# A recurrence's triangular inverses: systems on two partitions instead of one, and a load held back

## The chip, the cores and the metric

The kernel runs on one core of a Trainium2 chip. The core has a matrix engine (TensorE, PE in the rows), a vector engine (VectorE, DVE), an engine for activation functions and copies (ScalarE, ACT), a general one (GpSimd, POOL) and a queue engine that issues most DMAs (SyncE, SP). The metric is the device time of one execution in microseconds. Times of before: 2339.28 us, the median of 3 runs from 2338.95 to 2339.99.

## The reference, cut to what matters

The program is a decoder trunk of two layers with D = 2048 and T = 272 positions (256 and 16 learned ones): an RWKV-7 time mixing, a squared-ReLU MLP, a gated linear attention, another MLP. The change lies in the first mixer, whose recurrence over the positions is, for each of 32 heads of 64:

```python
def rwkv7_scan(r, w, k, v, a, b):
    def step(S, inp):
        r_t, w_t, k_t, v_t, a_t, b_t = inp
        sa = jnp.einsum('bhvk,bhk->bhv', S, a_t)
        S = S * w_t[:, :, None, :] + sa[..., None] * b_t[:, :, None, :] + v_t[..., None] * k_t[:, :, None, :]
        y = jnp.einsum('bhvk,bhk->bhv', S, r_t)
        return S, y
...
out = ((y + bonus).astype(x.dtype) * g) @ w_o
```

Around it stand projections of 2048 by 2048: keys and values before it, the output projection behind it.

## The kernel before, in words

The recurrence is computed in chunks of 64 positions (four, and a short fifth), in two groups of 16 heads. In a chunk, the positions depend on one another through a triangular system with a unit diagonal, for each head. `scores` (L956 on TensorE, masked on VectorE at L719 into a tile AM) makes these systems, and stores their diagonal blocks of 32 by 32 to DRAM (`sysd`, L963). `invert(b)`, b = 0 to 3, loads a batch of them into `sysA`, one system on each partition (L982: 64 of them for b = 0 and 2; 80 for b = 1 and 3, which have the short chunk too), and inverts all at once on VectorE in 30 steps. A step has two operations, both through the helper of L719: `upd` gets the product of a column and a row, and is then added into `sysA`. Step s works on s rows of 31 − s columns. Afterwards the inverses are stored (`invd`, L993), four transposes (L995, STREAM_TRANSPOSE) put some of them into `t11`, a part of `sysA`'s own tile, and loads from `invd` (L1000) put the rest into AM. `merge` joins two blocks of 32 to an inverse of 64 on TensorE (L1126, L1136).

All this runs beside projections that fill TensorE: each float32 product is split in three passes (L173 to L175), with a weight tile `raw` loaded by SyncE (`wload`, L141), rounded to `hi` by ScalarE (L150), and subtracted to `lo` by VectorE (L151), here in two halves of 512 columns. A pass with `lo` can't start before this subtraction. `R(n)` lets n units of the projections run (one unit is three matmuls), `until(n)` runs them up to a count, `MARK` holds the counts at which an inverse has to be there. `some(inv, n)` advances an inverse by n steps in the program's text.

The order on TensorE is that of the text (`manual_schedule`). That on the other engines is made by the framework's scheduler from its own costs, with priorities that the text gives (`high_priority`), so an inverse's steps are dealt out among VectorE's other work. Each engine then runs its instructions strictly in that order.

In the first inverse, `rest(f)` (L1044 on) prepares the keys of 128 channels, f = 0 to 15: decayed operands `bk` and `ar`, in two buffers each, are stored to DRAM (`bkd`, `ard`, L1008), and a buffer can be rewritten when its store has landed. `sums` (L1023) adds squares over channels on TensorE. The first inverse runs with f = 13, 14, 15 and the first value projections. The second group's start has the fourth inverse: `centre(1, 0)` puts the centred values `uv` (L1157), `norm` (L1247 to L1282) normalizes what came out of the first group, `outQ` adds partial sums of the output projection from psum into `r` and `hres` (`r<-pj` in the rows).

Of the kernel before, what the change touches and what calls it, by code (L numbers as in the profile page):

```python
# [13 lines left out]
ALU = mybir.AluOpType  # L14
# [4 lines left out]
P = 128  # L19
# [42 lines left out]
class Kern:  # L62
# [654 lines left out]
    def rwkv(self, done):  # L717
        nc, tc, ap = self.nc, self.tc, self.ap
        tt = lambda o, a, b, op=ALU.mult: nc.vector.tensor_tensor(out=o, in0=a, in1=b, op=op)  # L719
        hres = self.hres  # L720
# [5 lines left out]
        sysd, invd = ([self.t(self.dp, [112, 32, 32], f"{n}{b}") for b in range(4)] for n in ("sysd", "invd"))  # L726
# [27 lines left out]
        def hl(mt, xm):  # L754
            nc.scalar.copy(mt[:, 0], xm)
            tt(mt[:, 1], xm, mt[:, 0].bitcast(F32), ALU.subtract)
# [28 lines left out]
        with tc.manual_schedule(engines={ENG.PE, ENG.DVE, ENG.Activation}):  # L785
            for _ in range(2):
                nc.tensor.matmul(idle, warm[:, :128], warm[:, :512], start=True, stop=True)
            for i in range(8):
                sq, h = self.t(ep, [P, 2, T], "x", KT), d[:, 2 * i : 2 * i + 2]
# [8 lines left out]
            w = warm.bitcast(F32R)  # L798
            x, o = self.weave(w[:, :512]), self.pairs(idle)
# [37 lines left out]
            for kt in range(KT):  # L837
                w = weight(kt)
# [14 lines left out]
                p = parts.pop(0)  # L853
# [117 lines left out]

        def invert(b):
            X = sysA
            n = P if b % 2 else 64
            some_rows = [slice(0, 64), slice(96, 112)][: 1 + b % 2]
            if b % 2:
                nc.gpsimd.memset(X[64:96], 0.0)
            for rows in some_rows:  # L980
                with tc.high_priority(offset=4000):
                    nc.sync.dma_start(X[rows], sysd[b][rows])  # L982
            nc.gpsimd.memset(X[:n].rearrange("p a b -> p (a b)")[:, ::33], 1.0)
            yield
            for s in range(1, 31):
                k, m = 31 - s, s
                w = self.t(lp, [P, 240], "upd", 1)[:n, : k * m].rearrange("p (a b) -> p a b", a=m)
                tt(w, X[:n, s : s + 1, s + 1 :].to_broadcast([n, m, k]), X[:n, :m, s : s + 1].to_broadcast([n, m, k]))
                tt(X[:n, :m, s + 1 :], X[:n, :m, s + 1 :], w, ALU.add)
                yield  # L990
            for rows in some_rows:
                with tc.high_priority(offset=4000):
                    nc.sync.dma_start(invd[b][rows], X[rows])  # L993
            for k in (slice(8 * i, 8 * i + 8) for i in range(4)):
                nc.vector.transpose(t11.rearrange("p c h s -> p s c h")[:, k], X[0:32, k])  # L995
                yield
            for c in ((2, 3, 4) if b % 2 else (0, 1)):
                for rows, x in reversed(blocks(c, slice(0, 16))):
                    with tc.high_priority(offset=4000):
                        nc.sync.dma_start(x, invd[b][rows].rearrange("h s t -> s h t"))  # L1000
# [71 lines left out]
        with tc.manual_schedule(engines={ENG.PE}):  # L1072
            for f in range(KT):
                ps = (self.pry if f % 3 == 2 else self.pj)()[:, :T]
                keyproj(f, ps, 0)
                if f:
                    with tc.high_priority(offset=600):
                        rest(f - 1)
                keyproj(f, ps, 1)
                front(f, ps)  # L1080
                if f == 1:
                    xv = [self.t(self.xp, [P, 2, T], "x", KT, F32R) for _ in range(KT)]
                    for kt in range(KT):
                        hl(xv[kt], d[:, kt])
                    early2.close()
                    wl = ExitStack()
                    lp = wl.enter_context(tc.tile_pool(name="wl", bufs=1, reuse_waits="tile"))
                    BKs, ARs = ([self.t(lp, [P, 8, 256], n)] for n in ("BK0", "AR0"))
                    BKs.append(self.t(lp, [P, 8, 320], "BK1"))
                    AMs, AMrs = [self.t(lp, [P, 2, 16, 128], "AM0")], []  # L1090
                    sysA = self.t(lp, [P, 32, 32], "sysA")
                    t11 = sysA.rearrange("p a b -> p (a b)")[64:96].rearrange("p (c h s) -> p c h s", c=2, h=16)
                    nc.gpsimd.memset(sysA, 0.0)
                if f in (5, 6, 7):
                    dst, src, i, j = ((BKs[0], bkd, 0, 256), (ARs[0], ard, 0, 256), (BKs[1], bkd, 256, 576))[f - 5]
                    nc.sync.dma_start(dst[:, :4], src[:4, :, i:j].rearrange("f p n -> p f n"))
                if 8 < f < 13:
                    scores(0, (f - 9) // 2, (f + 1) % 2)
                if f == 12:
                    inv = invert(0)  # L1100
                if f > 12:
                    for _ in range(6):
                        next(inv, None)

        bank = lambda x: x.rearrange("p (h v) -> p h v", h=8)
        uvs, ras, bkts, rys, pSs = {}, {}, {}, {}, {}
# [39 lines left out]
        def centre(g, c):  # L1146
            full, n, nr = geom(c)[:3]
            pv = self.pm()
            for p in range(4):
                for e in range(2):  # L1150
                    nc.tensor.matmul(pv[64 * e : 64 * e + nr, p * P : (p + 1) * P], hres[:, 8 * g + 4 * e + p, c * C : c * C + nr],
                                     self.cent, start=True, stop=True)
            x = uvs[g, c] = self.t(kp, [P, 16, 64], "uv", 2)
            if not full:
                nc.gpsimd.memset(x[0 : 2 * n], 0.0)
            for e in range(2):
                nc.scalar.copy(x[:nr, 8 * e : 8 * e + 8], pv[64 * e : 64 * e + nr].rearrange("p (h v) -> p h v", h=8))  # L1157
# [219 lines left out]
        def R(n):  # L1377
            for _ in range(n):
                if next(work, work) is not work:
                    ran[0] += 1  # L1380
# [4 lines left out]
        def some(it, n):  # L1385
            for _ in range(n):
                next(it, None)
# [3 lines left out]
        self.split_parts = 2  # L1391
        ahead()
        with tc.manual_schedule(engines={ENG.PE}):
            R(4)
            with tc.high_priority(offset=600):
                rest(KT - 1)
            R(12)
            sums(None)
        early.close()

# [1 line left out]
        kp = win.enter_context(tc.tile_pool(name="win", bufs=1, side="right", reuse_waits="tile"))  # L1402
        ARs.append(self.t(kp, [P, 8, 320], "AR1"))
        AMs.append(self.t(kp, [P, 2, 16, 128], "AM1"))
        AMrs.append(self.t(kp, [64, 16, 64], "AMr"))
        sb = self.t(kp, [P, 8, HEAD], "S")
        for i in ((0, 128), (128, 320)):
            fetch(1, ARs, ard, i)
        with tc.manual_schedule(engines={ENG.PE}):
# [5 lines left out]
            for g in range(2):  # L1415
# [12 lines left out]
                m = merge(2 * g)  # L1428
# [1 line left out]
                some(last, 1)  # L1430
                R(4)
                next(m)
                inv = invert(2 * g + 1)
                some(inv, 3)
                until(128 + 128 * g)
                centre(g, 0)
                some(last, 1)
                R(2)
                keys(g, 0)
# [7 lines left out]
                for c in range(5):  # L1447
                    if c == 2:
# [5 lines left out]
                        m = merge(2 * g + 1)  # L1454
# [25 lines left out]
                    if g == 0 and c == 2:  # L1480
                        scores(2, 1, 1)
                        inv = invert(2)
# [351 lines left out]
```

## Time and profile before

| | us |
|---|---|
| median of 3 runs | 2339.28 |
| profiled execution | 2338.84 |
| its span | 2337.0 |
| TensorE busy in it | 2309.4 (99%) |
| VectorE busy | 1827.2 (78%) |
| ScalarE busy | 1381.9 (59%) |
| GpSimd busy | 311.8 (13%) |

The table is read against the bound: an engine that is busy for 99% of the span leaves little to be won, and only where it waits. The averages of the other engines say little of one stage: VectorE, at 78% of the whole, is nearly full in parts of the recurrence (about 240 to 500 us). A wait is given in brackets behind the instruction that waited, with the instruction that ended it.

### The profile page before, as it was taken

The numbers are of one execution on the slowest core, as the hardware profiler recorded it, in microseconds if no ns is written. First come the engines' busy times: TensorE is split into PE (matmuls) and PEld (weight loads), VectorE is DVE, ScalarE is ACT, GpSimd is POOL, SyncE is SP. The second block draws the span as 40 slices with busy tenths as digits, with TensorE's granted clock in tenths as the row PEclk, the third lists the DMA queues.
The fourth block names the chain that finished last, engine by engine and source line by source line (L and its number), as shares of the span: only waits on it lengthen the run. The fifth ranks groups of instructions, "written<-read, shape, count | busy, mean of one in ns | idle before, by whom it ended". The sixth has DMA issues, their size and how long they took to land.

```text
span 2337.0 us, 49154 instructions
## 1 busy us (share of the span) xinstructions
PE 2309.4 (99%) x19189; PEld 2178.4 (93%) x19189; DVE 1827.2 (78%) x3003; ACT 1381.9 (59%) x2176; POOL 311.8 (13%) x617
## 2 busy tenths in 40 slices
PE   9999999999999999999999999999999999999998
PEld 8888888889999999999999999999999898998997
DVE  8868976848677677767767787777768989989888
ACT  6488645556555445445435565556577777777776
POOL 0000000000144444444440011000000000000000
PEclk9999999999999999999999999999999999999999
DMA  6459754535799999999996666555657778777885
GB/s 213 161 193 314 242 163 146 155 90 168 248 330 333 317 332 327 325 324 324 326 336 232 202 224 205 171 173 182 211 192 264 269 266 267 274 266 264 276 288 199
DMA packets 202154, 571.97 MB, mean 245 GB/s; under 512 B 41473, under 2 KB 57601, under 8 KB 201793
## 3 DMA queue, kind: packets, MB, share of 16 engines
q1 hardware_dynamic: 174080, 477.58, 60.0%
q0 software_dynamic: 27840, 91.25, 12.4%
q8 instruction: 151, 2.47, 0.4%
q14 instruction: 83, 0.67, 0.1%
HBM read 507.00 MB, written 60.03 MB: 243 GB/s over the span
## 4 chain that ended last, share of the span: by engine, by line
PE 85%; DVE 10%; ACT 3%; issue 1%; DMA 1%; SPq 0%; DVEq 0%; ACTq 0%
PE pj L173 16%; PE pj L175 16%; PE pj L174 16%; PE pj L419 10%; PE pj L420 5%; PE pj L206 2%; DVE lo L151 2%; PE pj L207 1%; PE pu L508 1%; PE pu L509 1%; PE pu L510 1%; PE pt L510 1%; PE pt L508 1%; PE pt L509 1%; DVE upd L719 1%
## 5 line engine op out<-in xcount | busy, mean ns | idle before, releaser
L150 ACT CAST hi<-raw 128x1024 fp32r<-128x1024 f32 (+1 forms) x562 | 526.2, 947 | 593.7 <-PE pj L174 533.8
L151 DVE TENSOR_TENSOR lo<-raw,hi 128x1024 fp32r<-128x1024 f32 (+1 forms) x562 | 613.1, 1100 | 221.7 <-ACT hi L150 216.9
L173 PE MATMUL pj<-x,hi 128*128 128x272 f32 (+1 forms) x2560 | 730.3, 285 | 2.0 <-DVE r L719 0.9
L175 PE MATMUL pj<-x,lo 128*128 128x272 f32 (+1 forms) x2560 | 716.6, 280 | 4.4 <-DVE lo L151 4.1
L174 PE MATMUL pj<-x,hi 128*128 128x272 f32 (+1 forms) x2560 | 715.5, 279 | 0.0
L173 PEld LDWEIGHTS pj<-x,hi 128*128 128x128 f32 x2560 | 486.7, 190 | 14.8 <-issue 6.7
L175 PEld LDWEIGHTS pj<-x,lo 128*128 128x128 f32 x2560 | 486.7, 190 | 6.9 <-DVE lo L151 6.5
L174 PEld LDWEIGHTS pj<-x,hi 128*128 128x128 f32 x2560 | 486.8, 190 | 2.5 <-issue 1.4
L373 DVE TENSOR_TENSOR lo<-raw,hi 128x1024 fp32r<-128x1024 f32 x368 | 408.6, 1138 | 67.3 <-ACT hi L680 65.6
L680 ACT CAST hi<-raw 128x1024 fp32r<-128x1024 f32 x368 | 355.2, 980 | 112.6 <-PE pj L419 32.1
L419 PE MATMUL pj<-x,hi 128*128 128x512 f32 x1024 | 339.5, 383 | 0.0
L173 PE MATMUL pj<-h,hi 128*128 128x272 f32 x1024 | 286.2, 280 | 0.0
L175 PE MATMUL pj<-h,lo 128*128 128x272 f32 x1024 | 286.2, 280 | 0.0
L174 PE MATMUL pj<-h,hi 128*128 128x272 f32 x1024 | 286.2, 279 | 0.0
L420 PE MATMUL pj<-x,lo 128*128 128x256 f32 x1024 | 279.4, 273 | 0.0
L419 PEld LDWEIGHTS pj<-x,hi 128*128 128x128 f32 x1024 | 194.1, 190 | 26.3
L420 PEld LDWEIGHTS pj<-x,lo 128*128 128x128 f32 x1024 | 196.7, 192 | 1.8 <-DVE lo L373 0.2
L174 PEld LDWEIGHTS pj<-h,hi 128*128 128x128 f32 x1024 | 194.0, 189 | 0.0
L173 PEld LDWEIGHTS pj<-h,hi 128*128 128x128 f32 x1024 | 194.0, 189 | 0.0
L175 PEld LDWEIGHTS pj<-h,lo 128*128 128x128 f32 x1024 | 194.0, 189 | 0.0
L359 POOL DMA_DIRECT2D diff<-x x174 | 93.5, 543 | 12.6 <-DVE x L352 5.1
L345 POOL DMA_DIRECT2D x<-w_d x174 | 93.0, 541 | 2.8 <-issue 2.6
(370 smaller groups left out, 3537.9 us busy)
## 6 DMA issues: line engine op xcount, KB each, us to landing
raw<-mlp_w_d SPq DMA_DIRECT2D x384, 512.0 KB, 6.3
raw<-gla_in_d SPq DMA_DIRECT2D x98, 512.0 KB, 3.3
x<-w_d POOLq DMA_DIRECT2D x174, 256.0 KB, 7.0
diff<-x POOLq DMA_DIRECT2D x174, 256.0 KB, 8.9
raw<-w_rkv_d SPq DMA_DIRECT2D x80, 512.0 KB, 4.1
raw<-w_d SPq DMA_DIRECT2D x67, 512.0 KB, 4.5
raw<-diff SPq DMA_DIRECT2D x57, 512.0 KB, 5.3
raw<-gla_o_d SPq DMA_DIRECT2D x32, 512.0 KB, 3.3
```

The lines of the kernel that those rows point to most:

```text
L150: nc.scalar.copy(hi[:, h], raw[:, h])
L151: nc.vector.tensor_tensor(out=lo[:, h], in0=raw[:, h], in1=hi[:, h].bitcast(F32), op=ALU.subtract)
L173: nc.tensor.matmul(out, hi[:, ws], xh, start=first, stop=False)
L174: nc.tensor.matmul(out, hi[:, ws], xl, start=False, stop=False)
L175: nc.tensor.matmul(out, lo[:, ws], xh, start=False, stop=last)
L206: nc.tensor.matmul(wide, hi[:, ws], xt, start=kt == 0, stop=False)
L345: nc.gpsimd.dma_start(x[:, body], w[:, k])
L359: nc.gpsimd.dma_start(self.diff[b, g, i][:, k], x[:, body])
L373: tt = lambda o, a, b, op: nc.vector.tensor_tensor(out=o, in0=a, in1=b, op=op)
L419: nc.tensor.matmul(wide, hi[:, ws], xt, start=kt == 0, stop=False)
L420: nc.tensor.matmul(narrow, lo[:, ws], xt[:, 0], start=False, stop=kt == KT - 1)
L680: nc.scalar.copy(hi, raw)
```

## The change

In the first and third inverse each system now lies on two partitions, so that 128 work instead of 64. Partition half h = 0 has rows 0 to 3 of every 8 of the matrix that is built (X), h = 1 has rows 4 to 7. Each half also has a full copy of the system (L, in `sysA`), from which a step takes its row. A step s then covers 4 floor(s/8) + min(s mod 8, 4) rows of X instead of s. X of the first inverse lies in two blocks of `hres`, X of the third in a new tile `sysX`. There are two loads of the full systems and two of the halves for one load before, two stores for one, in pieces of 512 bytes, and the ones on the diagonal are set by GpSimd at the end of the steps instead of the start. The transposes read X.

The fourth inverse gets a `mark`: GpSimd first copies two elements for each partition of `uv` of the second group's first chunk into `sysA`, so that its main load waits for that copy. It begins behind `centre(1, 0)` in the text. Two counts change around the last `rest`: `R(7)` for `R(4)`, and `R(14)` for `R(12)`. TensorE's sum for it comes 9 matmuls later, the one of the pair behind it 5 units later in all; the rest of TensorE's order is as it was.

```diff
--- before.py
+++ after.py
@@ -971,28 +971,47 @@
 
 
 
-        def invert(b):
-            X = sysA
-            n = P if b % 2 else 64
-            some_rows = [slice(0, 64), slice(96, 112)][: 1 + b % 2]
-            if b % 2:
+        def invert(b, mark=None):
+            split = b % 2 == 0
+            sysX = halves[b // 2]
+            L, X = sysA, sysX[:, :512].rearrange("p (a b) -> p a b", a=16) if split else sysA
+            rows = [slice(0, 64), slice(64, 128) if split else slice(96, 112)]
+            fours = lambda x: x.rearrange("n (q h r) t -> n h q r t", q=4, h=2)
+            if not split:
+                if mark is not None:
+                    nc.gpsimd.tensor_copy(X[:64, 0, :2], mark)
                 nc.gpsimd.memset(X[64:96], 0.0)
-            for rows in some_rows:
+            for h in range(2):
                 with tc.high_priority(offset=4000):
-                    nc.sync.dma_start(X[rows], sysd[b][rows])
-            nc.gpsimd.memset(X[:n].rearrange("p a b -> p (a b)")[:, ::33], 1.0)
+                    nc.sync.dma_start(L[rows[h]], sysd[b][rows[0] if split else rows[h]])
+                    if split:
+                        nc.sync.dma_start(X[rows[h]].rearrange("n (q r) t -> n q r t", q=4), fours(sysd[b][rows[0]])[:, h])
+            if not split:
+                nc.gpsimd.memset(X.rearrange("p a b -> p (a b)")[:, ::33], 1.0)
             yield
             for s in range(1, 31):
-                k, m = 31 - s, s
-                w = self.t(lp, [P, 240], "upd", 1)[:n, : k * m].rearrange("p (a b) -> p a b", a=m)
-                tt(w, X[:n, s : s + 1, s + 1 :].to_broadcast([n, m, k]), X[:n, :m, s : s + 1].to_broadcast([n, m, k]))
-                tt(X[:n, :m, s + 1 :], X[:n, :m, s + 1 :], w, ALU.add)
+                k, m = 31 - s, s if not split else 4 * (s // 8) + min(s % 8, 4)
+                w = self.t(lp, [P, 240], "upd", 1)[:, : k * m].rearrange("p (a b) -> p a b", a=m)
+                tt(w, L[:, s : s + 1, s + 1 :].to_broadcast([P, m, k]), X[:, :m, s : s + 1].to_broadcast([P, m, k]))
+                tt(X[:, :m, s + 1 :], X[:, :m, s + 1 :], w, ALU.add)
                 yield
-            for rows in some_rows:
+            if split:
+                for h in range(2):
+                    nc.gpsimd.memset(sysX[rows[h]].rearrange("p (q z) -> p q z", q=4)[:, :, 4 * h : 4 * h + 100 : 33], 1.0)
+            for h in range(2):
                 with tc.high_priority(offset=4000):
-                    nc.sync.dma_start(invd[b][rows], X[rows])
+                    if split:
+                        nc.sync.dma_start(fours(invd[b][rows[0]])[:, h], X[rows[h]].rearrange("n (q r) t -> n q r t", q=4))
+                    else:
+                        nc.sync.dma_start(invd[b][rows[h]], X[rows[h]])
+            t = t11.rearrange("p c h s -> p s c h")
             for k in (slice(8 * i, 8 * i + 8) for i in range(4)):
-                nc.vector.transpose(t11.rearrange("p c h s -> p s c h")[:, k], X[0:32, k])
+                if split:
+                    h, q = k.start // 16, k.start // 8 % 2
+                    to = t11.rearrange("p c h (q g r) -> p g q r (c h)", q=4, g=2)[:, h, 2 * q : 2 * q + 2]
+                    nc.vector.transpose(to, X[64 * h : 64 * h + 32, 8 * q : 8 * q + 8])
+                else:
+                    nc.vector.transpose(t[:, k], X[0:32, k])
                 yield
             for c in ((2, 3, 4) if b % 2 else (0, 1)):
                 for rows, x in reversed(blocks(c, slice(0, 16))):
@@ -1089,6 +1108,7 @@
                     BKs.append(self.t(lp, [P, 8, 320], "BK1"))
                     AMs, AMrs = [self.t(lp, [P, 2, 16, 128], "AM0")], []
                     sysA = self.t(lp, [P, 32, 32], "sysA")
+                    halves = [hres[:, 8:10].rearrange("p a t -> p (a t)")]
                     t11 = sysA.rearrange("p a b -> p (a b)")[64:96].rearrange("p (c h s) -> p c h s", c=2, h=16)
                     nc.gpsimd.memset(sysA, 0.0)
                 if f in (5, 6, 7):
@@ -1391,10 +1411,10 @@
         self.split_parts = 2
         ahead()
         with tc.manual_schedule(engines={ENG.PE}):
-            R(4)
+            R(7)
             with tc.high_priority(offset=600):
                 rest(KT - 1)
-            R(12)
+            R(14)
             sums(None)
         early.close()
 
@@ -1404,6 +1424,7 @@
         AMs.append(self.t(kp, [P, 2, 16, 128], "AM1"))
         AMrs.append(self.t(kp, [64, 16, 64], "AMr"))
         sb = self.t(kp, [P, 8, HEAD], "S")
+        halves.append(self.t(kp, [P, 544], "sysX"))
         for i in ((0, 128), (128, 320)):
             fetch(1, ARs, ard, i)
         with tc.manual_schedule(engines={ENG.PE}):
@@ -1430,10 +1451,13 @@
                 some(last, 1)
                 R(4)
                 next(m)
-                inv = invert(2 * g + 1)
-                some(inv, 3)
+                if g == 0:
+                    inv = invert(1)
+                    some(inv, 3)
                 until(128 + 128 * g)
                 centre(g, 0)
+                if g:
+                    inv = invert(3, uvs[g, 0][:64, 0, :2])
                 some(last, 1)
                 R(2)
                 keys(g, 0)
```

Three places where the order on an engine moves. First SyncE, where the first inverse's systems are loaded (`sysA`, and `hres` behind the change) among weight tiles (`raw`) and the stores of prepared keys (`ard`, `bkd`), before:

```order
L141 DMA raw_3421<-w_rkv_d 128x1024
L982 DMA sysA_2014<-sysd_7_81 64x1024
L1008 DMA ard_80<-ar_1790 128x576
L141 DMA raw_3474<-w_rkv_d 128x1024
L1008 DMA bkd_79<-bk_1788 128x576
L141 DMA raw_3494<-w_rkv_d 128x1024
L1008 DMA ard_80<-ar_1791 128x576
L1008 DMA bkd_79<-bk_1789 128x576
L141 DMA raw_3556<-w_rkv_d 128x1024
```

and behind the change:

```order
L141 DMA raw_3423<-w_rkv_d 128x1024
L986 DMA sysA_2014<-sysd_7_81 64x1024 x2
L988 DMA hres_72<-sysd_7_81 64x4x128 x2
L141 DMA raw_3476<-w_rkv_d 128x1024
L141 DMA raw_3496<-w_rkv_d 128x1024
L1027 DMA ard_80<-ar_1790 128x576
L1027 DMA bkd_79<-bk_1788 128x576
L141 DMA raw_3558<-w_rkv_d 128x1024
L1027 DMA ard_80<-ar_1791 128x576
L141 DMA raw_3593<-w_rkv_d 128x1024
L1027 DMA bkd_79<-bk_1789 128x576
```

The two new loads stand ahead, and the first store of `ard` and of `bkd` now stand behind two weight loads and the second `bkd` behind two more, where before the first `bkd` stood behind one.

Next VectorE, at the end of the first inverse: the last steps, the subtractions `lo` of three weight tiles and the masking into AM, before:

```order
L719 TENSOR_TENSOR upd_3885<-sysA_2014 64x58
L719 TENSOR_TENSOR AM_612_3592<-pt_3868,cst_125 128x4x128
L719 TENSOR_TENSOR AM_612_3592<-pt_3869,cst_125 128x4x128
L719 TENSOR_TENSOR sysA_2014<-sysA_2014,upd_3885 64x29x2
L719 TENSOR_TENSOR upd_3888<-sysA_2014 64x30
L719 TENSOR_TENSOR sysA_2014<-sysA_2014,upd_3888 64x30
L151 TENSOR_TENSOR lo_3915<-raw_3912,hi_3914 128x512 x2
L995 STREAM_TRANSPOSE sysA_2014<-sysA_2014 32x8x32 x4
L151 TENSOR_TENSOR lo_3970<-raw_3967,hi_3969 128x512 x2
```

and behind the change, where `hres` is X:

```order
L719 TENSOR_TENSOR upd_3888<-sysA_2014,hres_72 128x32
L719 TENSOR_TENSOR hres_72<-hres_72,upd_3888 128x16x2
L719 TENSOR_TENSOR upd_3891<-sysA_2014,hres_72 128x16
L719 TENSOR_TENSOR hres_72<-hres_72,upd_3891 128x16
L1012 STREAM_TRANSPOSE sysA_2014<-hres_72 32x2x4x32 x2
L151 TENSOR_TENSOR lo_3860<-raw_3857,hi_3859 128x512 x2
L719 TENSOR_TENSOR r_18_92<-r_18_92,hres_72 128x272
L1012 STREAM_TRANSPOSE sysA_2014<-hres_72 32x2x4x32 x2
L719 TENSOR_TENSOR AM_616_3618<-pt_3871,cst_125 128x4x128
L719 TENSOR_TENSOR AM_616_3618<-pt_3872,cst_125 128x4x128
L151 TENSOR_TENSOR lo_3921<-raw_3918,hi_3920 128x512 x2
```

Before, the masking stood among the last steps, then came the `lo` of the next tile, and the transposes behind it. Now the steps and the transposes are all ahead of the masking and of that `lo` (3921, before 3915), with the preceding `lo` between the transposes (3860; its counterpart 3857 stood ahead of the rows shown).

Last VectorE, at the end of the fourth inverse: the last two steps, and the partial sums of the output projection that are read from psum (`r<-pj`), before:

```order
L719 TENSOR_TENSOR upd_6418<-sysA_2014 128x58
L719 TENSOR_TENSOR sysA_2014<-sysA_2014,upd_6418 128x29x2
L719 TENSOR_TENSOR upd_6471<-sysA_2014 128x30
L719 TENSOR_TENSOR sysA_2014<-sysA_2014,upd_6471 128x30
L995 STREAM_TRANSPOSE sysA_2014<-sysA_2014 32x8x32 x4
L719 TENSOR_TENSOR r_17_91<-pj_6518,r_17_91 128x272
L719 TENSOR_TENSOR r_18_92<-pj_6519,r_18_92 128x272
L151 TENSOR_TENSOR lo_6654<-raw_6651,hi_6653 128x512 x2
```

and behind the change:

```order
L719 TENSOR_TENSOR upd_6480<-sysA_2014 128x58
L719 TENSOR_TENSOR sysA_2014<-sysA_2014,upd_6480 128x29x2
L719 TENSOR_TENSOR upd_6483<-sysA_2014 128x30
L719 TENSOR_TENSOR r_17_91<-pj_6525,r_17_91 128x272
L719 TENSOR_TENSOR sysA_2014<-sysA_2014,upd_6483 128x30
L1014 STREAM_TRANSPOSE sysA_2014<-sysA_2014 32x8x32 x4
L719 TENSOR_TENSOR r_18_92<-pj_6526,r_18_92 128x272
L151 TENSOR_TENSOR lo_6666<-raw_6663,hi_6665 128x512 x2
```

One of the two psum readers has moved ahead of the last addition, the other stays behind the transposes.

## Rows read from the trace of the kernel before

**Rows 1.** The page: span, and busy time of the engines.

```profile
span 2337.0 us, 49154 instructions
...
PE 2309.4 (99%) x19189; PEld 2178.4 (93%) x19189; DVE 1827.2 (78%) x3003; ACT 1381.9 (59%) x2176; POOL 311.8 (13%) x617
```

**Rows 2.** Busy time by stage: stretch, length, busy us (x instructions) by engine, PEclk, DMA share, GB/s.

```profile
240.00:300.00 60.00, 57.72 (x507) 52.86 (x507) 57.22 (x153) 36.22 (x74) 1.26 (x4) 1.00 0.75 234
600.00:700.00 100.00, 100.00 (x866) 100.00 (x865) 70.05 (x92) 52.12 (x75) 36.36 (x75) 1.00 0.87 293
```

**Rows 3.** What TensorE waited for, 235 to 520 us: total us, times, longest.

```profile
PE pt L956 <- DVE AM L719: 2.7, 7, 0.7
PE pj L175 <- DVE lo L151: 2.4, 2, 1.8
PE pm L1023 <- ACT sq L1039: 1.7, 3, 0.8
```

**Rows 4.** Busy time by stage, 304 to 308 us; the clock stands behind POOL's count.

```profile
304.00:308.00 4.00, 4.00 (x27) 3.78 (x25) 3.97 (x9) 0.00 (x0) 0.00 (x0) 0.57 0.68 194
```

**Rows 5.** VectorE's groups by form, 240 to 500 us: busy us, mean ns, idle before.

```profile
...
L719 DVE TENSOR_TENSOR upd<-sysA 64x240 f32<-64x240 f32 x4 | 1.6, 397 | 0.1
...
L719 DVE TENSOR_TENSOR upd<-sysA 128x150 f32<-128x150 f32 x4 | 1.3, 315 | 0.1
...
L719 DVE TENSOR_TENSOR upd<-sysA 128x30 f32<-128x30 f32 x4 | 0.8, 197 | 0.1
L719 DVE TENSOR_TENSOR upd<-sysA 64x30 f32<-64x30 f32 x4 | 0.8, 191 | 10.0 <-DMA sysA<-sysd 9.9
```

**Rows 6.** Timeline of VectorE, 302 to 305 us: start, length, instruction [idle before].

```profile
302.08 1.28 DVE L151 TENSOR_TENSOR lo<-raw,hi 128x512 fp32r<-128x512 f32 x2
303.40 1.92 DVE L995 STREAM_TRANSPOSE sysA<-sysA 32x256 f32<-32x256 f32 x4
```

**Rows 7.** Timeline of VectorE and SyncE, 256 to 265 us.

```profile
256.14 0.44 SPq L1008 DMA_DIRECT2D bkd<-bk  x1
259.40 0.33 SPq L141 DMA_DIRECT2D raw<-w_rkv_d  x1
...
258.02 0.18 DVE L719 TENSOR_TENSOR upd<-sysA 64x30 f32<-64x30 f32 x1 [0.56 <-DMA sysA<-sysd]
264.11 0.50 DVE L719 TENSOR_TENSOR bk<-kn,iW 128x256 f32<-128x256 f32 x2
```

**Rows 8.** One tile's instructions, bkd: last line, the landing of its transfers.

```profile
DMA to landing us min/median/max: 3.2/5.6/8.7
```

**Rows 9.** DMA, 383 to 393 us: GB/s in 40 slices; issues with KB and landing.

```profile
GB/s 33 36 132 28 108 7 67 61 46 229 220 287 343 384 374 364 394 353 379 404 384 394 396 494 342 179 109 10 32 20 20 38 16 16 0 66 0 0 0 0
...
BK<-bkd SPq DMA_DIRECT2D x1, 1280.0 KB, 7.8
sysA<-sysd SPq DMA_DIRECT2D x1, 256.0 KB, 6.9
```

**Rows 10.** Timeline of VectorE and TensorE, 391 to 423 us.

```profile
391.93 0.18 DVE L719 TENSOR_TENSOR upd<-sysA 64x30 f32<-64x30 f32 x1 [9.33 <-DMA sysA<-sysd]
...
408.27 0.49 PE L956 MATMUL pt<-AR,BK 64*128 64x128 f32 x2 [0.28 <-DVE AM L719]
...
422.26 1.14 PE L956 MATMUL pt<-AR,BK 64*64 64x64 f32 x30 [0.50 <-DVE AM L719]
```

**Rows 11.** Timeline of VectorE, ScalarE and TensorE, 441 to 479 us.

```profile
441.20 0.18 DVE L719 TENSOR_TENSOR upd<-sysA 128x30 f32<-128x30 f32 x1
441.48 1.17 ACT L1157 COPY uv<-pm 64x512 f32<-64x512 f32 x2 [0.68 <-PE pm L1151]
...
476.33 1.98 DVE L995 STREAM_TRANSPOSE sysA<-sysA 32x256 f32<-32x256 f32 x4
...
478.84 0.38 PE L173 MATMUL pj<-x,hi 128*128 128x272 f32 x1 [0.95 <-DVE r L719]
```

**Rows 12.** One line's instructions, L982: last line, the landing of the inverses' loads.

```profile
DMA to landing us min/median/max: 2.7/4.7/6.9
```

## The prediction

> **What bounds the kernel now.** I read first the busy time of the engines, then the busy time by stage, then what TensorE waits for in the recurrence, then the single instructions around those waits. TensorE is busy for 2309.4 of 2337.0 us [rows 1], so the idle time that any change can win is 27.6 us, and from 600 to 700 us it is busy for 100.00 of 100 us [rows 2]: nothing there absorbs a delay, and what the recurrence (about 240 to 500 us) gains or loses arrives at the end whole. From 240 to 300 us TensorE stands still for 60 − 57.72 = 2.3 us while VectorE is busy for 57.22 of 60 us [rows 2]. VectorE runs the four inverses in the gaps of its other work, and TensorE follows it there: between 235 and 520 us TensorE waited 2.7 us for the masking of scores (AM), 2.4 us for the low half of a weight tile (lo, one wait of it 1.8 us) and 1.7 us for ScalarE's squares [rows 3]. Behind the long lo wait comes a second cost: from 304 to 308 us the granted clock was 0.57 [rows 4], so 4 us were worked at close to the lower level of 1.2 GHz; at the mean of 0.57 the work done was 2.3 us' worth, so 1.7 us are lost.
>
> The profiled execution took 2338.84 us, 1.84 us more than its span; the median of the runs is 2339.28, 0.44 us above it. I form differences against the profiled one and add them to the median.
>
> **The shorter steps.** A step s of an inverse is two VectorE operations over m rows by 31 − s columns. With m = s the elements of the 30 steps add up to 4960 per operation; with m = 4 floor(s/8) + min(s mod 8, 4) to 2960. On 64 partitions 30 elements took 191 ns and 240 took 397 ns; on 128 partitions 30 took 197 ns and 150 took 315 ns [rows 5]. Both give (397 − 191)/210 = (315 − 197)/120 = 0.98 ns for an element, and a part that does not shrink of 191 − 29 = 162 ns or 197 − 29 = 168 ns. An inverse on 64 partitions is now 60 x 162 ns + 9920 x 0.98 ns = 19.4 us; split it is 60 x 168 ns + 5920 x 0.98 ns = 15.9 us. VectorE gains 3.5 us in the first inverse and 3.5 us in the third. It cannot gain more, since the 60 operations stay. The page "VectorE: DVE Perf Modes" of the Trainium skill (section "The TRN2 errata") gives an fp32 operation as its elements plus 151 cycles at 0.96 GHz; the same arithmetic would make it 19.8 and 15.6 us, a gain of 4.2 us. The rows slope less (0.98 against 1.04 ns), and I keep the rows. That section's rule, a cost per instruction that only larger operations spread, speaks against this change, which makes operations smaller, and the rows agree: 162 to 168 ns of each remain.
>
> **First inverse.** The lo subtraction that TensorE waited longest for ran at 302.08, since it stands behind the last steps and a masking in VectorE's order; four transposes follow it, 1.92 us in all [rows 6]. In the new order two transposes, another lo, a sum and two more transposes all stand ahead of the masking, and only then comes the lo in question. VectorE is earlier by the 3.5 us and by the 0.56 us that its first step waited for the load [rows 7] (that step now stands behind more work), and later by the 1.92 us of transposes: 2.1 us ahead on this count. The masking waits for TensorE's own scores, so not all of it is usable; of the 2.4 us of lo waits I take 1.7.
>
> Against this stands SyncE's queue. The four loads (768 KB for 256 KB) stand where one did, and the stores of two bk blocks have moved behind a weight load each. The first was issued at 256.14, and can now be issued no earlier than the weight load at 259.40; such a store took 3.2 to 8.7 us to land, median 5.6 [rows 7, 8]. VectorE overwrites the same block at 264.11 [rows 7]. With the median, 259.4 + 5.6 = 265.0, so it is held 0.9 us; the next block, pushed back in the same way, adds a little, and I take 1.3 us together. By the least landing it is nothing, by the longest 259.4 + 8.7 − 264.1 = 4.0 us. The first inverse thus nets 1.7 − 1.3 = 0.4 us, with ends of +2.4 and −4.0 + 1.7 = −2.3.
>
> The later sums of the last block (rest(15)) remove one of the three waits of 1.7 us for ScalarE's squares [rows 3], about 0.6 us, but TensorE then only comes sooner to the same lo, which VectorE sets. I count nothing, with an upper end of 0.6.
>
> The half clock I count as gone, +1.7 us: what ends the stretch ahead of it is one stall of 1.8 us, and this is split into shorter ones. By the Trainium skill ("TensorE: Matmul & The Clock Gate", section "HAM oscillation"), it is gaps in TensorE's work that bring the clock down. The trace agrees as far as that the fall stands right behind its longest wait. That a shorter wait keeps the clock up no row shows; otherwise this term is nothing.
>
> **Third inverse.** Its load of 256 KB took 6.9 us behind a load of 1280 KB, which took 7.8, and VectorE stood idle 9.33 us for it until 391.93 [rows 9, 10]. The change adds 512 KB. At the 1280 KB's rate that is 512/1280 x 7.8 = 3.1 us; at the 350 to 400 GB/s that the middle of this stretch shows [rows 9] it is 1.3 to 1.5 us. I take 1.5, since the stretch was moving bytes at that rate when the load stood in it. The steps start 1.5 us later, and run 3.5 us shorter, so VectorE is 1.5 us behind at first and 2.0 ahead at the end. The waits for AM, 2.7 us in 7 places [rows 3], lie between 408 and 423 us [rows 10], past the middle of the inverse, where most of the gain has been made. I take 1.5 us of the 2.7; with 3.1 us for the load it is 0.3, and with none late 2.7. Pieces of 512 bytes are the least that the Trainium skill ("DMA: Bandwidth & Descriptors", "Specifications") gives full rate; by it the new loads cost as their bytes do, and no row here has such pieces.
>
> **Fourth inverse.** Its first step ran at 441.20. The load now waits for ScalarE's uv copy of 441.48 (its second half is not waited for) and a small GpSimd copy behind it, say until 442.8; such loads took 2.7 to 6.9 us, median 4.7 [rows 11, 12]. A load in an emptier queue should be short of the median: I take 3.7, so a first step at 446.5, 5.3 us later. On SyncE the loads of g2 and of the residual stand behind the waiting load; they are prefetches with time in hand. VectorE does the other work of this stretch first, and idles about 3.7 us for it; of the 5.3 us some 2.5 are not made up, since until 478 it has little slack. Transposes then start at about 478.8 instead of 476.33. In the new order one psum reader (r_17) is ahead of them and one (r_18) behind. TensorE already waited 0.95 us for these readers at 478.84 [rows 11]. With the second reader behind the transposes it waits 2.5 us longer than before for that bank, less the 1.0 us in which it still has the first bank to fill: −1.5 us. Landing after 2.7 us makes it −0.5; after 6.9 us, 3.2 us more, −4.7.
>
> **Sum:** 0.4 + 1.7 + 1.5 − 1.5 = 2.1 us gained. 2339.28 − 2.1 = 2337.2 us. About 0.2%, 4.7 us here, is what a measurement tells from no change; 2.1 us lie within it.
>
> **Rivals.** *All of it pays.* No store holds VectorE, the clock stays up, the fourth inverse is off TensorE's path: 2.4 + 1.7 + 2.7 = 6.8 us, 2332.5 us. For it: VectorE gains 7 us just where TensorE waits for it. Against it: each gain has its own new wait in front.
> *The held load decides.* The fourth load lands after the longest time, 6.9 us: −4.7 us, and the longer stall at 480 us brings the clock down as at 304 us, −1.7. With 0.4 + 1.5 from the first and third inverse and the old half clock gone for 1.7: −2.8 us, 2342.1 us; with the third load late as well (1.2 less) 2343.3. It decides from a landing about 1.5 us past my 446.5, where its loss eats the rest. For it: this load took 6.9 us in the third inverse; against: there it had 1280 KB ahead.
> *The stores hold the first inverse.* Both stores land late: 4.0 us of hold; the lo wait is then as long as before and the half clock stays: −2.3 + 1.5 − 1.5 = −2.3 us, 2341.6 us. For it: three more loads stand in front of these stores. Against: the median landing is 5.6 us.
> *The operations do not get shorter,* because twice the partitions cost what half the rows save. 197 against 191 ns [rows 5] speaks clearly against it. Then only the moves remain: 0.4 − 1.7 for the first inverse, 0 − 1.5 for the fourth: 2342.
>
> **Chances.** My forecast 0.55, all of it pays 0.17, held load 0.13, stores 0.12, no shorter operations 0.03. The range runs from 2333.3 to 2341.5: it holds the forecast's spread of some 3 us and about half of each rival. Faster by over 0.2% (below 2334.6): nearly all of the first rival and the forecast's lower tail, 0.18. Slower by over 0.2% (above 2344.0) only if late landings add up: 0.06. Within: 0.76.
>
> **What would show it.** Steps right: the upd operations with 16 to 152 elements at 168 ns + 0.98 ns for each; TensorE's wait for lo near 300 us under 1 us and no clock under 1 from 300 to 310 us; a VectorE wait of about 1 us ahead of a bk write near 264 us; AM waits of about 1.2 us between 405 and 425 us; the fourth inverse's first step near 446.5 us and a wait for r near 479 us of 2 to 2.5 us. Wrong: a low clock that has moved to another place, a wait for the third load past 395 us, or an unchanged lo wait, which would say that not VectorE's load but the masking's own scores set it.

## The result and the profile after

The changed kernel takes 2342.06 us (median of 22 runs, 2340.74 to 2345.92), the kernel before 2338.2 (22 runs, 2336.5 to 2339.99): a ratio of 1.0019, with a 95% interval from 1.0012 to 1.0025. It is 3.9 us slower, where 2.1 us faster were forecast, and lies 0.6 us above the upper end of the range. The forecast started from 2339.28 us, the median of three runs, which the 22 runs put 1.1 us lower.

The page of the changed kernel, span and engines, to hold beside [rows 1]:

```profile
span 2341.3 us, 49172 instructions
...
PE 2310.4 (99%) x19189; PEld 2176.4 (93%) x19189; DVE 1822.0 (78%) x3003; ACT 1382.6 (59%) x2176; POOL 312.9 (13%) x620
```

Its busy time by stage, for [rows 2, 4], the last three lines being the stretches in which the clock now falls:

```profile
240.00:300.00 60.00, 57.95 (x508) 52.70 (x504) 55.73 (x158) 37.11 (x75) 1.38 (x6) 1.00 0.80 249
304.00:308.00 4.00, 3.19 (x32) 2.94 (x33) 4.00 (x8) 1.01 (x3) 0.00 (x0) 1.00 0.51 90
600.00:700.00 100.00, 100.00 (x863) 99.92 (x862) 69.29 (x91) 52.45 (x75) 35.70 (x72) 1.00 0.86 285
...
490.00:492.00 2.00, 2.00 (x16) 1.75 (x20) 0.44 (x1) 0.95 (x3) 0.00 (x0) 0.74 0.59 225
492.00:494.00 2.00, 2.00 (x60) 2.00 (x62) 0.00 (x0) 0.01 (x1) 0.00 (x0) 0.50 0.00 0
494.00:496.00 2.00, 2.00 (x22) 1.85 (x18) 0.44 (x1) 1.82 (x4) 0.00 (x0) 0.91 0.00 0
```

TensorE is as full as before behind the recurrence. At 304 to 308 us the clock is up, but it falls between 490 and 496 us: 0.52 + 1.00 + 0.18 = 1.7 us lost, as much as before at the other place.

What TensorE waits for, for [rows 3] (total us, times, longest):

```profile
PE pj L175 <- DVE lo L151: 3.8, 5, 1.5
PE pj L173 <- DVE r L719: 2.3, 2, 1.4
PE pt L956 <- DVE AM L719: 1.6, 5, 0.4
PE pt L1156 <- DMA AM<-invd: 1.3, 1, 1.3
```

The waits for AM fell from 2.7 to 1.6 us and those for ScalarE's squares are gone. But the waits for lo rose from 2.4 to 3.8 us, those for r from 0.9 to 2.3, and one for a reload of AM is new. Of the waits for lo, these three are the longest:

```profile
275.76 0.38 PE L175 MATMUL pj<-x,lo 128*128 128x272 f32 x1 [1.48 <-DVE lo L151]
...
300.85 0.38 PE L175 MATMUL pj<-x,lo 128*128 128x272 f32 x1 [0.93 <-DVE lo L151]
...
304.81 0.38 PE L175 MATMUL pj<-x,lo 128*128 128x272 f32 x1 [0.92 <-DVE lo L151]
```

The one wait of 1.8 us near 303 us [rows 3] has become two, which together are as long. The steps' operations, for [rows 5]:

```profile
L719 DVE TENSOR_TENSOR upd<-sysA,hres 128x152 f32<-128x152 f32 x1 | 0.3, 318 | 0.0
...
L719 DVE TENSOR_TENSOR upd<-sysA,hres 128x16 f32<-128x16 f32 x1 | 0.2, 188 | 0.0
```

The fourth inverse, for [rows 11], on GpSimd, SyncE, VectorE and TensorE:

```profile
441.69 0.18 POOL L982 COPY sysA<-uv 64x2 f32<-64x2 f32 x1 [7.31 <-ACT uv L1177]
441.90 0.49 SPq L986 DMA_DIRECT2D sysA<-sysd  x1
...
446.23 0.19 DVE L719 TENSOR_TENSOR upd<-sysA 128x30 f32<-128x30 f32 x1 [0.16 <-issue]
...
478.03 0.38 PE L173 MATMUL pj<-x,hi 128*128 128x272 f32 x1 [1.38 <-DVE r L719]
478.12 1.95 DVE L1014 STREAM_TRANSPOSE sysA<-sysA 32x256 f32<-32x256 f32 x4
480.10 0.44 DVE L719 TENSOR_TENSOR r<-pj,r 128x272 f32<-128x272 f32 x1
480.60 0.38 PE L173 MATMUL pj<-x,hi 128*128 128x272 f32 x1 [0.91 <-DVE r L719]
481.77 0.34 SPq L141 DMA_DIRECT2D raw<-rw_oA_d  x1
482.20 1.45 SPq L1019 DMA_DIRECT2D AM<-invd  x3
...
484.22 1.02 SPq L1019 DMA_DIRECT2D AM<-invd  x1
...
488.76 0.92 PE L1156 MATMUL pt<-AM,rs 32*32 32x32 f32 x46 [1.31 <-DMA AM<-invd]
```

The load goes out behind the copy of uv at 441.9, the first step runs at 446.23, 5 us later than before. The transposes begin at 478.1, the second reader of psum (r) ends behind them, and the last load that puts the inverses back into AM goes out at 484.2 and is waited for until 488.76. These reloads don't stand behind the late stores alone: a weight tile (`raw`) goes out at 481.77, ahead of them. In the kernel before, all of the reloads went out ahead of it:

```profile
481.29 0.49 SPq L1000 DMA_DIRECT2D AM<-invd  x1
481.87 6.60 SPq L141 DMA_DIRECT2D raw<-rw_oA_d  x3
```

The landing of the reloads into AM from their issue, before and then changed:

```profile
DMA to landing us min/median/max: 1.8/2.6/3.2
```

```profile
DMA to landing us min/median/max: 4.0/4.1/4.5
```

So the last reload went out 2.9 us later than before, and took about 1.5 us longer to land.

One execution of each kernel is a small basis for 3.9 us, so two more traces were taken of each. The table has the time that TensorE took from one matmul to another that both kernels have: from the scores at 244.90 us (L956, by the first trace of before) to the first merge at 322.16 (L1126), from there to the product `pu<-uv,AM` of the second group at 448.40 (L1175), and from there to `pry<-AR,S` at 500.26 (L1201). A low clock within a stage is included.

| us | before, three traces | mean | changed, three traces | mean |
|---|---|---|---|---|
| 244.90 to 322.16 (first inverse) | 77.26, 74.96, 75.07 | 75.76 | 75.76, 75.96, 75.04 | 75.59 |
| 322.16 to 448.40 (third) | 126.24, 125.81, 125.94 | 126.00 | 124.62, 124.72, 125.18 | 124.84 |
| 448.40 to 500.26 (fourth) | 51.86, 51.84, 51.86 | 51.85 | 56.75, 55.15, 56.71 | 56.20 |
| of it lost to a low clock | 1.7, 0, 0 | 0.57 | 1.7, 0, 1.7 | 1.13 |

The first split gained next to nothing (0.2 us), the third 1.2 us, and in the stage of the fourth inverse 4.3 us were lost. There, the lost clock is 1.7 us in two of the changed kernel's three traces; before, it is the first trace's in the first stage.

### The profile page after: what moved, and what is told of

Its sections match the earlier page's. It is cut to its first block, busy times and chain, and to the rows that moved or that the text cites. A ratio compares the mean times of both kernels' runs of the same rounds, so it can differ in the third digit from the quotient of the medians.

```text
span 2341.3 us, 49172 instructions
## 1 busy us (share of the span) xinstructions
PE 2310.4 (99%) x19189; PEld 2176.4 (93%) x19189; DVE 1822.0 (78%) x3003; ACT 1382.6 (59%) x2176; POOL 312.9 (13%) x620
## 4 chain that ended last, share of the span: by engine, by line
PE 84%; DVE 9%; ACT 3%; issue 2%; DMA 1%; SPq 0%; DVEq 0%; ACTq 0%
PE pj L173 16%; PE pj L175 16%; PE pj L174 16%; PE pj L419 10%; PE pj L420 5%; PE pj L206 2%; DVE lo L151 2%; PE pj L207 1%; PE pu L508 1%; ACT hi L150 1%; PE pu L509 1%; PE pu L510 1%; PE pt L510 1%; PE pt L509 1%; PE pt L508 1%
```

## The experiments

**The four parts.** Theory: the held load costs 4 to 5 us, the splits gain. Rival: the splits' transfers cost it. Each part stands alone on the kernel before, or is taken from the change. All ratios are to the kernel before as it ran beside each group: 2338.47 us for this group, 2338.17 for the next four kernels, 2338.22 for the last two.

```diff
 no_hold: the change, with
-                if g == 0:
-                    inv = invert(1)
-                    some(inv, 3)
+                inv = invert(2 * g + 1)
+                some(inv, 3)
...
-                if g:
-                    inv = invert(3, uvs[g, 0][:64, 0, :2])
 hold_only: the kernel before, with this part of the change alone
 first_only, third_only: no_hold, with
-            split = b % 2 == 0
+            split = b == 0          (third_only: b == 2, and R(4), R(12))
```

> The whole change except the held load: the fourth inverse's load is issued where it was before. Theory 'hold' (the late fourth inverse costs 4 to 5 us through the psum readers, the reload of AM and the half clock behind them, while the two splits gain about 3 us): 3 us below the kernel before, about 2335, no wait for the reload of AM near 488 us and no clock under 1 there. Rival 'split' (the splits' extra transfers and moved stores cost the 4 us, the hold nothing): as slow as the whole change, about 2342. Third possibility: the fourth inverse's steps, now free to start earlier, stand in VectorE's order ahead of two lo subtractions and wait there for their load; then TensorE waits for lo at 430 to 440 us and 1 to 3 us of the gain are lost again, about 2337.

2342.28 us, 1.0018 (1.0009 to 1.0027): the change's loss, without the hold. The third possibility comes nearest, but the wait stands at another place (third_only, below).

> The kernel before with the held load alone. Theory 'hold': 4 to 5 us slower than before, about 2343, with a first step of the fourth inverse near 446 us, about 2.3 us of waits for r near 479 us, a wait of about 1.3 us for the reload of AM, and a low clock behind it. Rival 'split': no slower than before, 2338.

2343.06 us, 1.0019 (1.0010 to 1.0028): 4.6 us slower, as the theory said. One of its parts did not come: this kernel's trace has no wait for the reload of AM (rows below). Its reloads stand ahead of the weight tile, as before, and land in 1.9 to 2.7 us; in their place stand a longer wait for r, 1.0 us more for uv, and a low clock from 479.2 to 482.6 us.

> The kernel before with the first inverse split and the two counts of units that go with it. Theory 'hold': 1 us faster than before (the traces of before and after show TensorE 1.2 us further on at 311 us than at 255 us), about 2337, with no low clock at 304 to 308 us. Rival 'split' (the late stores of bk hold VectorE, and the lo waits only move): 1 to 2 us slower, about 2340.

2338.75 us, 1.0001 (0.9992 to 1.0010): neither gain nor loss.

> The kernel before with the third inverse split alone. Theory 'hold': 1.5 us faster at 422 us than before; at the end that, if the fourth inverse's steps do not stand in the way, about 2336.7, and up to 2 us worse if they do, since they then start earlier in VectorE's order. Rival 'split' (the longer load makes VectorE late): 1 us slower, about 2339.

2342.88 us, 1.0016 (1.0007 to 1.0025): 4.4 us slower. Neither simple story holds: the hold alone costs 4 us, and so does the third split without it. The waits of TensorE in hold_only, then in third_only, show two different places:

```profile
PE pj L173 <- DVE r L719: 2.9, 1, 2.9
PE pj L175 <- DVE lo L151: 2.4, 2, 1.8
PE pm L1269 <- ACT uv L1159: 1.7, 1, 1.7
```

```profile
PE pt L1290 <- DVE hres L1301: 3.6, 1, 3.6
PE pj L175 <- DVE lo L151: 2.6, 3, 1.8
```

With the hold, the readers of psum wait (2.9 us). Without it, with VectorE free sooner, the scheduler puts the fourth inverse's steps ahead of the casts, lo and norm of the second group, and TensorE waits 3.6 us in one piece for norm's result (L1301). VectorE's timeline of third_only there:

```profile
432.45 0.19 DVE L719 TENSOR_TENSOR upd<-sysA 128x30 f32<-128x30 f32 x1 [0.65 <-POOL sysA L982]
...
439.63 0.38 DVE L719 TENSOR_TENSOR upd<-sysA 128x210 f32<-128x210 f32 x1
439.93 1.29 DVE L151 TENSOR_TENSOR lo<-raw,hi 128x512 fp32r<-128x512 f32 x2
...
446.49 0.49 DVE L1301 SCALAR_TENSOR_TENSOR hres<-r,vecs,pt 128x272 f32<-128x272 f32 x1
```

Steps run from 432.45 us on, the lo that TensorE needs at 439.93, norm's last operation at 446.49. In the kernel before, the first step ran at 441.20 only [rows 11]. In third_only's execution the clock was 0.50 to 0.56 from 446 to 456 us as well; in no_hold's, which has the same wait (3.3 us), it stayed up (third_only, then no_hold):

```profile
450.00:452.00 2.00, 2.00 (x31) 1.75 (x32) 1.46 (x5) 0.20 (x1) 0.00 (x0) 0.50 0.46 135
```

```profile
450.00:452.00 2.00, 2.00 (x43) 1.53 (x43) 1.97 (x6) 1.16 (x3) 0.00 (x0) 1.00 0.72 204
```

**The hold on the step instead of the load.** If the late load is the cost, and the order the reason for having a hold at all, then the first step has to be held, and the load not.

```diff
 load_early: the change, with
-                    nc.gpsimd.tensor_copy(X[:64, 0, :2], mark)        (ahead of the loads)
+                    nc.gpsimd.tensor_copy(self.t(lp, [P, 240], "upd", 1)[:64, :1], mark[:, :1])   (behind them)
-                    inv = invert(3, uvs[g, 0][:64, 0, :2])
+                    inv = invert(3, rr[KT - 1][:64])
 third_early: third_only, with the same hold
```

> The whole change, but the fourth inverse's load is free again and only its first step is held, until the last value projection has been added into r (GpSimd touches the step's buffer behind that addition). Theory 'late load' (of the 4 us that the change costs, the fourth inverse's late steps make 2.5 to 4 through the psum readers, the reload of AM and a low clock behind): the first step runs at about 441 to 442 us, the waits for r near 479 us fall to 1 us, none for the reload; 2338 to 2339, level with before, since the first inverse's split still costs 1 us and the third's gains 1. Rival 'order' (what counts is that VectorE's order has changed, whenever the load comes): still 2341 to 2342.

2338.01 us, 1.0001 (0.9992 to 1.0010). The loss is gone, with both splits in place.

> The kernel before with the third inverse split, and the fourth inverse's first step (not its load) held until the last value projection has been added into r. Theory 'late load': the third split's gain of about 1.1 us (AM waits 1.8 for 2.7 us, none for S) stays to the end: 2337, 1 us below before, and 5 us below the third split alone, whose fourth inverse started too early in VectorE's order and held up norm by 3.6 us. Rival 'order': 2339 to 2342.

2337.39 us, 0.9996 (0.9987 to 1.0005): third_only lay 4.4 us above the kernel before, this lies 0.8 below, which the interval does not tell from none. load_early's waits of TensorE, and its fourth inverse on VectorE:

```profile
PE pj L173 <- DVE r L719: 0.9, 1, 0.9
PE pt L956 <- DVE AM L719: 1.7, 5, 0.4
```

```profile
444.18 0.43 DVE L719 TENSOR_TENSOR r<-r,hres 128x272 f32<-128x272 f32 x1
444.89 0.19 DVE L719 TENSOR_TENSOR upd<-sysA 128x30 f32<-128x30 f32 x1 [0.28 <-POOL upd L989]
```

The step runs 0.7 us behind the addition that it is held for, with no wait for a DMA; r is waited for 0.9 us as before, the reload of AM not at all. By the traces this is the whole of the fourth inverse's loss: the stage from 448.40 to 500.26 us takes 51.85 us in load_early and 51.83 in third_early, as before (51.84 to 51.86). In the kernels that hold the load, it takes 55.15 to 56.75 in the changed one's three traces, 55.40 in hold_only.

**The reload, and the two counts.**

```diff
 mark_later: the change, with
-MARK = [120, 170, 244, 302]
+MARK = [120, 170, 244, 308]
 old_counts: the change, with
-            R(7)
+            R(4)
-            R(14)
+            R(12)
```

> The whole change with the second group's second merge 6 units (18 matmuls, 2.1 us) later. If the wait of 1.3 us for the reload of AM is a cost of its own: 1.3 us less than the whole change, about 2340.8, and the wait gone. If TensorE only meets the same lateness at another place: 2342.

2341.68 us, 1.0015 (1.0007 to 1.0024). The wait for the reload is gone in its trace, but the median fell by 0.4 us only, and less than the runs can tell; a wait of 0.7 us for a cast stands at 549.57 instead. Neither answer is clear. hold_only, whose reload is not waited for, is as slow by the median; of its eleven executions ten have a mean clock below 0.999 (12 of 33 of the kernel before), which points to the clock for more of its loss.

> The whole change with the two counts of units around the last block's sums as before. If these later sums cost what TensorE now waits for lo at 275.8 us (1.5 us): 1 us faster than the whole change, about 2341. If that wait comes from the stores of bk that land late, the counts change nothing, or the ScalarE wait of 0.6 us comes back: 2342 to 2343.

2342.29 us, 1.0018 (1.0009 to 1.0027): the counts change nothing; waits of 1.4 us for ScalarE's squares are back, and the lo waits are 0.4 us less than in the changed kernel. The squares are not a matter of the counts alone, though: load_early, with the new counts, waited 1.9 us for them.

**The stores in the first inverse.** VectorE's waits in first_only, and the lo wait of TensorE behind them:

```profile
DVE bk L719 <- DMA bkd<-bk: 1.2, 1, 1.2
DVE upd L719 <- DMA hres<-sysd: 0.9, 1, 0.9
```

```profile
275.95 0.38 PE L175 MATMUL pj<-x,lo 128*128 128x272 f32 x1 [2.06 <-DVE lo L151]
```

```diff
 stores_first: load_early; first_stores: first_only; both with, in store
+            elif f in (12, 13):
+                with tc.high_priority(offset=1800 if f == 12 else 1300):
+                    q.dma_start(dst[f], x)
```

> As load_early (both splits, the fourth inverse's load free, its first step held), with the stores of ard and bkd of f = 12 and 13 put back ahead of weight loads, with as many weight loads in front of each bkd store as in the kernel before or one fewer. Theory 'stores' (the first split loses its gain because VectorE waits about 1 us for a bkd store that stands behind weight loads, and TensorE then 1.5 to 2 us for lo near 276 us): VectorE's wait for bkd gone, the lo wait near 276 us under 0.7, about 1.5 us faster than load_early, 2336.6, below the kernel before. Rival 'load' (the 768 KB of the first split's load hold VectorE's first step and the rest behind it, the stores nothing): 2338 as load_early.

2337.39 us, 0.9995 (0.9986 to 1.0004): 0.6 below load_early, 0.8 below before.

> As first_only, with the same four stores put back ahead. Theory 'stores': no VectorE wait for bkd, the lo wait near 276 us under 0.7; 1.3 us faster than first_only, 2337.3. Rival 'load': 2338.7 as first_only.

2338.42 us, 0.9998 (0.9989 to 1.0007). VectorE's waits between 235 and 300 us in stores_first, and TensorE's:

```profile
DVE lo L151 <- ACT hi L150: 1.5, 3, 0.5
DVE upd L719 <- DMA hres<-sysd: 0.2, 1, 0.2
```

```profile
PE pj L175 <- DVE lo L151: 2.7, 5, 1.2
PE pt L956 <- DVE AM L719: 1.6, 5, 0.4
PE pm L1045 <- ACT sq L1061: 0.5, 1, 0.5
```

The wait for the store is gone, the one for the loads nearly so, and the lo waits fell from 4.1 us in load_early to 2.7; but load_early's traced execution took 2341.28 us, 3.3 above its median. The lo wait near 276 us is 0.6 us in stores_first and 0.85 in first_stores, where under 0.7 was expected. That the moved stores are a part of this wait is shown. They are not all of it: in the third trace of the changed kernel VectorE waits for no store, and TensorE still 0.98 us for that lo. Their worth in time, some 0.5 us, is less than the runs can tell.

**More traces of the two kernels.**

> A second trace of the changed kernel. If the low clock behind the late readers and the late reload is the rule: again 1.5 to 2 us lost to it between 478 and 496 us, and again 2.3 us of waits for r and over 1 us for the reload. If it was that one execution's: clock 1.00 there, and the 3.9 us must come from elsewhere.

> A second trace of the kernel before. If the low clock at 304 to 308 us follows its lo wait of 1.8 us: again 0.57 there. If it comes by chance (the same wait stood in three other traces, with a clock of 1.00 in two of them): as likely 1.00.

> A third trace of the changed kernel, with the same question: 1.5 to 2 us lost to a low clock between 478 and 496 us if that is the rule, none if not.

> A third trace of the kernel before, with the same question: 0.57 at 304 to 308 us if the lo wait brings it every time, 1.00 in about half of the executions if by chance.

The waits hold: r 2.3 us and the reload 1.2 us in both of the changed kernel (2343.26 and 2341.80 us), lo 2.4 and 2.3 us in both of before (2336.21 and 2339.84 us). The clock does not: between 478 and 496 us it fell in one of the two, at 304 to 308 us in neither. The second trace of before:

```profile
304.00:308.00 4.00, 4.00 (x38) 3.88 (x37) 3.97 (x9) 1.14 (x2) 0.00 (x0) 1.00 0.60 175
```

## Why the prediction was wrong

- *Shorter steps*: right. 152 elements took 318 ns and 16 took 188, for 317 and 184 by the formula.
- *First inverse, +0.4*: a loss rather than a gain. The three traces say 0.2 gained together with the clock; but over all eight traces with this split and the stores where it puts them, the stage took 76.5 us in the mean (75.0 to 77.8), in the six unsplit 75.7 (75.0 to 77.3), so 0.8 us more. The gain of 1.7 us on lo did not come: TensorE had waited once, for 1.8 us; now it waits twice, for 0.91 to 0.93 us each, in all three traces. The steps end earlier, but they and two of the transposes now stand ahead of the preceding lo (300.10 us on VectorE) as well, whose wait the sum did not price. It is not the scores that set the second one: the masking in front of it (302.87) waited for nothing. No run moves the transposes alone.
- *The stores, −1.3 in it*: VectorE waited for a store of bk only at the second block (near 273 us, not 264), 0.6, 0.5 and 0 us in the three traces. TensorE waited 1.48, 1.36 and 0.98 us for the lo behind it, a wait that the sum did not have. The landing was misread: [rows 8] also has four loads from bkd; the stores of L1008 alone took 3.2 to 7.4 us, so the longest hold would have been 2.7 us and not 4.0. And the second block moved behind two more weight loads, not one. The waits for squares, set at nothing, were 1.1 to 1.7 us in the six unsplit traces and 0 to 1.9 in the split ones: no clear gain.
- *Half clock gone, +1.7*: the failed step on the side of the gains. The clock did stay up there in every trace with the first split, but before it had not been down as a rule. The lo wait of 1.8 us stood in six traces of kernels with the first inverse unsplit in that place (three of before, hold_only, third_only, third_early), and the clock fell behind it in two. So the term belonged to one execution; the median of before contains it only in part. I should have priced it at a third. The mean granted clock of each execution fits this: of 87 of the kernel before, 29 have 0.998 and 58 have 0.999, and the 29 took 1.4 to 2.2 us longer, by group; it doesn't show where they lost it.
- *Third inverse, +1.5*: nearly right, 1.2 in the means of the table, and the waits for AM fell by 1.1 us in the first pair. The load cost as estimated: its first step ran at 393.90, 2.0 us later, for 1.5.
- *Fourth inverse, −1.5*: the step that failed and decided. Its parts up to the readers were right: first step at 446.23 (forecast 446.5), 2.3 us of waits for r (2 to 2.5); up to the merge at 483.90 the stage lost 1.8 us in all three traces. Missing was what comes behind: the reload of AM, which goes through DRAM behind the last step and now also stands behind a weight tile, and which the prediction does not name, a wait of 1.2 to 1.3 us; and the clock, which I had put into a rival only, 1.7 us in two of three traces. In all, 4.3 us in the means in place of 1.5. hold_only, with 4.6 us, and load_early, which takes the late load out and wins 4.0 us (2342.06 to 2338.01), agree that the late load alone is worth the loss.
- *Rivals*: "the held load decides" is what happened (2342.1 forecast, 2342.06 measured), but not by its condition: the load landed when I expected it. That its number fits so well is luck: it starts from a median 1.1 us too high, and credits 1.7 us for a low clock before that most executions did not have. By its own terms the load would have had to land 2.1 us past 446.5 to eat the rest, not 1.5. "The stores hold the first inverse" gives nearly the same number, 2341.6, but putting the stores back won only 0.6 us of load_early's time.
- What I did not see at all: the hold was not free to leave out. With the third split, the scheduler moves the fourth inverse's steps up and loses as much (no_hold, third_only). I compared the change with the order of before, not with its own order without the hold.

Open: by the table, 0.2 + 1.2 − 4.3 makes a loss of 2.9 us by 500 us, where the medians say 3.9. The three traces of the changed kernel came to the scores at 244.90 us 1.1 us later in the mean, but single traces of either kernel differ there by over 2 us, so this can't be told from chance. With the first inverse's −0.8 us from all traces in place of 0.2, the sum is −0.8 + 1.2 − 4.3 = −3.9 us. That it meets the medians so closely is luck, since the first stage varies by 2.7 us between the split kernels' traces, for a reason that stays open.

## What to carry to other kernels

When a step is made to start later, follow its results to their last consumer, reloads and their place in the DMA queue included: the first wait moved as computed, and more than half of the price stood behind it. If a load is held only to keep an engine's order, hold the first instruction that uses it, and let the load go early. A low clock that is seen in one execution is a chance, to be weighed by how many traces of the same wait show it.

## What the runs showed of the hardware

The same wait of TensorE, with the same work ahead and behind, is followed by the clock's lower level in some executions and not in others: 1.8 us at 303 us in two of six traces; 3.3 and 3.6 us at 447 us in one of two kernels, and there the low level lasted some 10 us and took 5.1 us.
